# More rows by seven products in the head and MLP products of a one-core encoder layer, one more sum per half carried by transfers, and two raw weight buffers

## The chip, the core and the metric

The program runs on one core of a Trainium2 chip (trn2). TensorE (PE in the profile, PEld for its weight loads) multiplies, VectorE (DVE) and ScalarE (ACT) work on tiles, GpSimd (POOL) and SyncE (SP) issue transfers; ACT issues a few too. The metric is the device time of one execution in microseconds (us).

## What is computed

One layer over 256 tokens of width 2048, all in float32: a retention mixer of 8 heads, a squared-ReLU MLP with 8192 hidden columns, a norm ahead of each and one at the end.

```python
hn = rmsnorm(x, norm1)
q, k, v, g = split(hn @ w_in)              # 8 heads: 256, 256, 512, 512 columns each
q, k = rotary(q), rotary(k) * 256**-0.5
o = retention over chunks of 64 (q k^T, decayed, times v, with a carried state)
x = x + (head_norm(o) * silu(g)) @ w_out   # 4096 -> 2048
h2 = rmsnorm(x, norm2)
x = x + square(relu(h2 @ w_up)) @ w_down   # 2048 -> 8192 -> 2048
out = rmsnorm(x, final_norm)
```

## The kernel before, in words

**Weights.** A weight arrives in float32 from memory. It is split on the chip in two parts: ACT copies it into a rounded tile `wh` (L72, L155) and DVE subtracts that from the raw weight into `wl` (L73, L156). Activations are held as two parts in the same way. A product is three matmuls for each 128 x 512 block of weights: high by high, high by low, low by high. There are four pairs of `wh`/`wl` buffers of 1024 columns. ACT may write a pair only when TensorE has used what was in it, and DVE comes after ACT.

**Regular blocks.** `load_block` (L62 to L85) brings 1 MB (128 x 2048) from memory into a `raw` buffer by a transfer on SP's queue and splits it in two pairs. There are three raw buffers. In `seven` such a block is the step `r`: two rows of 128 of the weight matrix, 24 matmuls.

**Seven products.** `seven` computes a product with 256 tokens and 1024 output columns. Part of the weight's rows go in pairs by Strassen's scheme: the four quarters b11, b12, b22, b21 of the weight are loaded (step `w`, L207), and seven products of sums of quarters (steps `1` to `7`) take the place of eight. A product of n pairs is 3n matmuls, and n pairs by seven products are 21n, where regular blocks take 24n. The quarters are summed in place between the products, each sum once the quarter that it overwrites has been split for the product that still needs it: step `a` is b11 += b12, `b` is b12 += b22, `c` is b11 += b22, `d` is b21 += b11. A sum is a DVE addition (L202) or a transfer that adds, issued by POOL (L200). Products that belong to several blocks of the result are added from PSUM by DVE (`sub_out`, L718; `add_residual`, L586).

The order of work in each half of columns is written out by hand as a string of steps. The tile framework's scheduler then orders each engine's queue; each engine runs its queue in order.

**Stages.** Heads (0 to about 560 us): head 0 by regular blocks; for heads 1 to 7 first the queries and keys (`queries`, 4 blocks), then gates and values in one `seven` (3 pairs and 5 regular blocks, all four sums by DVE). Then the output product, two halves with 4 pairs. Then the MLP in four quarters of 2048 hidden columns; a quarter is 16 blocks of the first product (`proj_cols`, L97 and L98, results squared and split into `hs`) and two halves of the second product, each a `seven` with 4 pairs and 4 regular blocks: `rw1abr5cr26dr374`, sums `b` and `d` by transfers and `a` and `c` by DVE. The quarters b11, b12 and b22 live in the tile `raw3`, b21 in `raw1`; each holds one half's weights, so a quarter's next load waits for its last reader. In the very last half the final norm (`finish`) runs between the products.

Of the kernel before, what the change touches and what calls it, by code (L numbers as in the profile page):

```python
# [15 lines left out]
P = 128  # L16
T = 256
# [8 lines left out]
EPS = 1e-6  # L26
NB = T // P
WARM = 8
SPR = 3
SPO = 4  # L30
SPM = 4
QT = 16
STRASSEN_HEADS = range(1, 8)


@with_exitstack
def trunk_kernel(ctx: ExitStack, tc: tile.TileContext, io, out):
# [19 lines left out]
    def tiles(t):  # L57
        return [t[:, k] for k in range(t.shape[1])]

    def load_block(src, rows, cols, lead=None):  # L62
        raw = wp.tile([P, 2048], F32, tag="raw", name="raw", bufs=3)
        if lead is None:
            nc.sync.dma_start(raw, src)
        parts = []
        for s in range(2):
            wh = wp.tile([P, 1024], F32R, tag="wh", name="wh", bufs=4)
            wl = wp.tile([P, 1024], F32R, tag="wl", name="wl", bufs=4)
            r = raw[:, s * 1024 : (s + 1) * 1024]  # L70
            if lead is None:
                nc.scalar.copy(wh, r)  # L72
                nc.vector.tensor_sub(wl, r, wh.bitcast(F32))  # L73
            for k in range(rows // 2):
                sl = slice(k * cols, (k + 1) * cols)
                if lead is not None:
                    row = s * rows // 2 + k
                    lead(row)
                    nc.sync.dma_start(r[:, sl], src[:, row * cols : (row + 1) * cols])
                    nc.scalar.copy(wh[:, sl], r[:, sl])  # L80
                    nc.vector.tensor_sub(wl[:, sl], r[:, sl], wh[:, sl].bitcast(F32))
                parts.append((wh[:, sl], wl[:, sl]))
        return parts
# [56 lines left out]
    def seven(quads, blocks, raws, xs, sx, sub_out, done, order, side, extra=None, np_=SPR, nk=QT, by_dma=()):  # L140
# [34 lines left out]
        def total(i):  # L175
            return lambda p: (sx[p][:, i, 0], sx[p][:, i, 1])

        def out(b, c, acc, sign):
            sub_out(b, c, acc, sign, (b, c) not in taken)
            taken.add((b, c))  # L180
# [15 lines left out]
                    add(kt, wh, wl, b, range(2), kt == nk - 1)  # L196

        def plus(to, other):
            if to in by_dma:
                nc.gpsimd.dma_start(w[to], w[other], accum_op=ALU.add)  # L200
            else:
                nc.vector.tensor_add(w[to], w[to], w[other])  # L202

# [30 lines left out]
        def p7():  # L234
            chain = other["s"]
            product(chain, "s", w["b12"], total(2))
            out(1, 0, chain, 1)
            out(1, 1, chain, -1)

        steps = {"w": whole, "1": p1, "2": p2, "3": p3, "4": p4, "5": p5, "6": p6, "7": p7, **(extra or {})}  # L240

# [9 lines left out]

        finished = set()
        steps["A"] = lambda: finish_at((0, 0), (0, 1))
        steps["B"] = lambda: finish_at((1, 1))
        g = 0
        for step in order:
            if step == "r":
# [21 lines left out]
    xs = cp.tile([P, KT, 2, T], F32R, tag="xs", name="xs")  # L279

    xr = cp.tile([P, KT, T], F32, tag="ya", name="xr", padded_shape=[P, 32, T])
    sraw = cp.tile([P, 4, SPR * 512], F32, tag="yb", name="sraw")
    sxc = cp.tile([P, 2, 4, 2, P], F32R, tag="yc", name="sxc")
    x0 = tiles(xs)
    ys = [None] * VT

# [34 lines left out]
    if True:  # L321
# [74 lines left out]
        def queries(h, fillers):  # L396
            acc = [bank("acc_qk", 0) for _ in range(4)]
            proj_cols(io["w_qk"][h], x0, acc, fillers, (lambda w: st.update(first=w)) if h == 0 else None)
            qk = ap.tile([P, 2, 2, T], F32, tag="qk", name="qk")
            for i in range(2):  # L400
                both = []
                for o in (2 * i, 2 * i + 1):
                    a = ap.tile([P, T], F32, tag="sum", name="sum", bufs=3)
                    nc.scalar.copy(a, acc[o][:, T:])
                    nc.vector.tensor_add(a, acc[o][:, :T], a)
                    both.append(a)
                a1, a2 = both
                t = [ap.tile([P, T], F32, tag="rot", name="rot", bufs=4) for _ in range(4)]
                nc.vector.tensor_mul(t[0], a1, cosr)
                nc.vector.tensor_mul(t[1], a2, sinr)  # L410
                nc.vector.tensor_mul(t[2], a1, sinr)
                nc.vector.tensor_mul(t[3], a2, cosr)
                nc.vector.tensor_sub(qk[:, i, 0], t[0], t[1])
                nc.vector.tensor_add(qk[:, i, 1], t[2], t[3])
            st["qk"] = qk
# [66 lines left out]

        def sums_x():

            sx3 = ap.tile([P, 4, 2, P], F32R, tag="xh", name="sx3", bufs=2)
            to = [sxc[:, 0], sxc[:, 1], sx3]
            for p in range(SPR):
                s = []
                for k in (2 * p, 2 * p + 1):
                    s.append(ap.tile([P, T], F32, tag="sum", name="sum", bufs=3))  # L490
                    nc.scalar.activation(s[-1], xr[:, k], AF.Copy, scale=norm1[:, k : k + 1])
                k = 2 * SPR + 2 * p
                u = xr[:, k : k + 2].rearrange("p a (s t) -> p (a s) t", s=2)
                sums(to[p], s, u)
            st["sx"] = to

        def gates_values(h):

            sg = ap.tile([P, NB, DV], F32, tag="sg", name="sg")
            vf = ap.tile([P, NB, DV], F32, tag="xh", name="vf", bufs=2)  # L500
            v = ap.tile([P, NB, 2, DV], F32R, tag="v", name="v")
            to = (sg, vf)

            def sub_out(b, c, bank, sign, first):
                t = to[c][:, b]
                if first:
                    nc.scalar.copy(t, bank)
                else:
                    nc.vector.tensor_tensor(t, t, bank, op=ALU.add if sign > 0 else ALU.subtract)

            def done(acc, b, c):
                t = to[c][:, b]
                nc.vector.tensor_add(t, t, acc[b][c])
                if c == 0:
                    nc.scalar.activation(t, t, AF.Silu, scale=rs[:, b : b + 1])
                else:
                    split_scaled(v[:, b], t, rs[:, b : b + 1])

            i = h - STRASSEN_HEADS[0]
            seven(  # L520
                io["w_gv_s"][i], io["w_gv_r"][i], [sraw[:, j] for j in range(4)], x0, st["sx"],
                sub_out, done, "rwr1abr5cr2d3s6r74", 1, extra={"s": lambda: scores(h)},
            )
            st["sg"], st["v"] = sg, v

        for h in range(H):
            if h == 0:
                gates(h, [], lead=lead_x)
                queries(
                    h,  # L530
                    [(0, lambda: square_tokens(0, 0)), (0, lambda: square_tokens(0, 1)), (0, load_constants)]
                    + [(g, lambda g=g: square_tokens(1, g - 1)) for g in (1, 2)]
                    + [(3, first_norm), (3, gate_silu)],
                )
                values(h, [(0, lambda: load_decay(0)), (1, lambda: load_decay(1)), (1, sums_x), (2, lambda: scores(0))])
                ys_part("ya", 0, 16)
            else:

                queries(h, [(1, lambda: mix(h - 1))] + ([(3, lambda: turn(h - 1))] if h <= 4 else []))
                if h + 1 < H:  # L540
                    load_decay(h + 1)
                gates_values(h)
        ys_part("yb", 16, 12)
        ys_part("yc", 28, 4)


    mp = None
# [101 lines left out]


    hs = tiles(cp.tile([P, QT, 2, T], F32R, tag="ya", name="hs"))
    raw3 = cp.tile([P, 3, SPM * 512], F32, tag="yb", name="raw3")
    raw1 = cp.tile([P, SPM * 512], F32, tag="yc", name="raw1")
    rs3 = mp.tile([P, NB], F32, name="rs3")

    def times_norm(b, q):
# [3 lines left out]
    def finish(acc, b, half, c):  # L660
# [15 lines left out]
        if c != b:  # L676
            r = rs3[:, b : b + 1]
            for q in range(4):
                n = slice(q * 512, (q + 1) * 512)
                if q % 2:  # L680
                    nc.scalar.activation(x[:, b, n], x[:, b, n], AF.Copy, scale=r)
                    nc.scalar.dma_start(out[b * P : (b + 1) * P, n], x[:, b, n])
                else:
                    nc.vector.tensor_scalar_mul(x[:, b, n], x[:, b, n], r)
                    nc.sync.dma_start(out[b * P : (b + 1) * P, n], x[:, b, n])
# [6 lines left out]
    for q in range(4):  # L692
# [21 lines left out]
        for half in range(2):  # L714

            def sub_out(b, c, acc, sign, first, half=half):
# [2 lines left out]

            last = q == 3  # L720
            seven(
                io["w_down_s"][q][half], io["w_down_r"][q][half], [raw3[:, j] for j in range(3)] + [raw1], hs, sx, sub_out,
                (lambda a, b, c, half=half: finish(a, b, half, c)) if last
                else (lambda a, b, c, half=half: add_residual(a, half, b, c)),
                "rw1abr5cFr2d36rA7B4" if last and half == 1 else "rw1abr5cr26dr374",
                1 - half, np_=SPM, extra={"F": first_half_times_norm}, by_dma=("b12", "b21"),
            )


# [95 lines left out]
```

## Time and profile before

| | |
|---|---|
| median of 3 runs | 1445.39 us (1445.39 to 1446.39) |
| the profiled execution's own time | 1445.77 us |
| its span, first to last instruction | 1444.0 us |
| busy share of the span: PE, DVE, ACT, POOL | 99%, 78%, 56%, 3% |
| mean granted TensorE clock | 0.998 of full speed |
| read from memory | 277.18 MB, 193 GB/s over the span |

Busy time of an engine is a share of the whole span; a stage can be fuller. Matmuls are pipelined: one of 512 columns is listed with some 0.39 us, but the next starts 0.23 us after it. So the cost of a matmul more or less is taken from stretches of many in a row, not from the mean of one.

### The profile page before, as it was taken

To read this page: it belongs to the slowest core of one execution; us is meant where nothing else is said; L and a number is where in the kernel's file an instruction comes from. 1 tells how busy PE (TensorE), PEld (TensorE's weight loads), DVE (VectorE), ACT (ScalarE), POOL (GpSimd) and SP (SyncE) were. 2 spreads that over 40 slices of the span, in tenths; PEclk is the share of its full clock that TensorE was granted. 3 is DMA by queue.
4 is the path that set the end of the run, shared out by engine and by line. 5 is a ranking of instruction groups with operands and counts; after the bars stand their busy time and mean duration, and the time that the engine had idled before them with its cause. 6 is when DMAs were issued, how large, how long until landed. Compare 5 with 4: busy or idle time off the path is not lost.

```text
span 1444.0 us, 18258 instructions
## 1 busy us (share of the span) xinstructions
PE 1431.0 (99%) x6985; PEld 1196.8 (83%) x6985; DVE 1132.5 (78%) x1494; ACT 807.3 (56%) x1067; POOL 41.4 (3%) x66
## 2 busy tenths in 40 slices
PE   9999999999999999999999999999999999999996
PEld 7888888888888888888888888888888888888885
DVE  6768888888788888889568688777887678867787
ACT  5655564646464556555546555556555555556564
POOL 2000000000000000000000000000000000000000
PEclk9999999999999999999999999999999999999999
DMA  9845555546464636563475577754876557865773
GB/s 327 331 150 188 179 195 175 188 169 213 166 234 137 231 132 245 205 248 103 164 290 193 185 219 218 271 197 153 270 245 224 187 169 243 284 209 175 208 230 87
DMA packets 45863, 297.23 MB, mean 206 GB/s; under 512 B 5344, under 2 KB 5888, under 8 KB 13776
## 3 DMA queue, kind: packets, MB, share of 16 engines
q1 hardware_dynamic: 41184, 271.60, 53.2%
q0 software_dynamic: 3872, 23.42, 7.4%
q8 instruction: 54, 0.88, 0.2%
q10 hardware_dynamic: 720, 1.06, 0.2%
q14 instruction: 33, 0.27, 0.1%
HBM read 277.18 MB, written 2.10 MB: 193 GB/s over the span
## 4 chain that ended last, share of the span: by engine, by line
PE 98%; issue 0%; DMA 0%; ACT 0%; DVE 0%; POOLq 0%; POOL 0%; SPq 0%
PE acc_d L161 43%; PE acc_u L97 17%; PE acc_s L161 9%; PE acc_u L98 8%; PE acc_qk L97 8%; PE acc_qk L98 4%; PE acc L161 3%; PE po L456 1%; PE pst L433 1%; PE acc_g L112 1%; PE acc_g L113 1%; PE acc_g L116 1%; PE acc_v L116 1%; PE acc_v L113 1%; PE acc_v L112 1%; PE pt L478 0%
## 5 line engine op out<-in xcount | busy, mean ns | idle before, releaser
L73 DVE TENSOR_TENSOR wl<-raw,wh 128x1024 fp32r<-128x1024 f32 x382 | 463.6, 1222 | 204.9 <-ACT wh L72 202.8
L72 ACT CAST wh<-raw 128x1024 fp32r<-128x1024 f32 x382 | 398.9, 1050 | 369.3 <-PE acc_d L161 153.8
L97 PE MATMUL acc_u<-x1s,wh 128*128 128x512 f32 x1024 | 362.4, 398 | 0.0
L98 PE MATMUL acc_u<-x1s,wl 128*128 128x256 f32 x1024 | 287.6, 281 | 0.0
L97 PEld LDWEIGHTS acc_u<-x1s,wh 128*128 128x128 f32 x1024 | 192.5, 188 | 47.3
L161 PE MATMUL acc_d<-wh,xs 128*128 128x512 f32 x644 | 206.6, 393 | 0.0
L161 PE MATMUL acc_d<-wh,hs 128*128 128x512 f32 x640 | 205.8, 395 | 0.0
L98 PEld LDWEIGHTS acc_u<-x1s,wl 128*128 128x128 f32 x1024 | 192.2, 188 | 0.2
L97 PE MATMUL acc_qk<-xs,wh 128*128 128x512 f32 x512 | 181.2, 397 | 0.0
L156 DVE TENSOR_TENSOR wl<-raw,wh 128x1024 fp32r<-128x1024 f32 x112 | 135.0, 1222 | 39.1 <-ACT wh L155 38.9
L155 ACT CAST wh<-raw 128x1024 fp32r<-128x1024 f32 x112 | 117.3, 1049 | 84.8 <-PE acc_d L161 62.7
L161 PEld LDWEIGHTS acc_d<-wh,xs 128*128 128x128 f32 x644 | 121.0, 188 | 27.3 <-issue 0.7
L161 PEld LDWEIGHTS acc_d<-wh,hs 128*128 128x128 f32 x640 | 120.6, 188 | 27.3
L98 PE MATMUL acc_qk<-xs,wl 128*128 128x256 f32 x512 | 143.1, 281 | 0.0
L161 PE MATMUL acc_d<-wl,xs 128*128 128x512 f32 x322 | 126.1, 392 | 0.0
L161 PE MATMUL acc_d<-wl,hs 128*128 128x512 f32 x320 | 125.6, 394 | 0.0
L155 ACT CAST wh<-sraw 128x1024 fp32r<-128x1024 f32 x98 | 80.5, 835 | 72.7 <-PE acc_d L161 50.6
L97 PEld LDWEIGHTS acc_qk<-xs,wh 128*128 128x128 f32 x512 | 95.8, 188 | 22.7
L156 DVE TENSOR_TENSOR wl<-sraw,wh 128x1024 fp32r<-128x1024 f32 x98 | 91.3, 955 | 24.0 <-ACT wh L155 23.2
L98 PEld LDWEIGHTS acc_qk<-xs,wl 128*128 128x128 f32 x512 | 96.1, 188 | 2.2 <-DVE wl L73 1.2
L161 PEld LDWEIGHTS acc_d<-wl,hs 128*128 128x128 f32 x320 | 60.3, 188 | 13.8
L161 PEld LDWEIGHTS acc_d<-wl,xs 128*128 128x128 f32 x322 | 60.5, 188 | 13.3
(195 smaller groups left out, 1830.8 us busy)
## 6 DMA issues: line engine op xcount, KB each, us to landing
raw<-in_w_up SPq DMA_DIRECT2D x64, 1024.0 KB, 4.9
raw<-in_w_gv_r SPq DMA_DIRECT2D x35, 1024.0 KB, 5.0
raw<-in_w_qk SPq DMA_DIRECT2D x32, 1024.0 KB, 5.0
raw<-in_w_down_s SPq DMA_DIRECT2D x32, 1024.0 KB, 5.2
raw<-in_w_down_r SPq DMA_DIRECT2D x32, 1024.0 KB, 5.1
raw<-in_w_o_r SPq DMA_DIRECT2D x24, 1024.0 KB, 5.0
sraw<-in_w_gv_s SPq DMA_DIRECT2D x28, 768.0 KB, 4.2
raw<-raw POOLq DMA_DIRECT2D x16, 1024.0 KB, 8.2
```

The costliest lines, as they stand in the source:

```text
L72: nc.scalar.copy(wh, r)
L73: nc.vector.tensor_sub(wl, r, wh.bitcast(F32))
L97: nc.tensor.matmul(acc, wh[:, c], both, start=(kt == 0), stop=False)
L98: nc.tensor.matmul(acc[:, :T], wl[:, c], xs[kt][:, 0, :], start=False, stop=(kt == KT - 1))
L112: nc.tensor.matmul(accs[b][c], xs[kt][:, 0, t], wh[:, n], start=(kt == 0), stop=False)
L113: nc.tensor.matmul(accs[b][c], xs[kt][:, 0, t], wl[:, n], start=False, stop=False)
L116: nc.tensor.matmul(accs[b][c], xs[kt][:, 1, t], wh[:, n], start=False, stop=(kt == nk - 1))
L155: nc.scalar.copy(wh[:, :n], c)
L156: nc.vector.tensor_sub(wl[:, :n], c, wh[:, :n].bitcast(F32))
L161: nc.tensor.matmul(to, x, w, start=(key not in begun), stop=last, skip_group_check=True)
L433: nc.tensor.matmul(pst[:, to], qk[:, 1, i, b * P : (b + 1) * P], qk[:, 0, i, q], start=(i == 0), stop=(i == 1))
L456: nc.tensor.matmul(po, s, w, start=(n == 0), stop=(n == len(terms) - 1))
```

## The change

Heads 1 to 7: four pairs by seven products and four regular blocks (before: three and five), and step `b` goes to a transfer. Second MLP product: five pairs and three regular blocks in each half (before: four and four), quarters of 128 x 2560, and the sums `b`, `c` and `d` go by transfers (before: `b` and `d`), each in two pieces of 1280 columns (5120 bytes) a row. From head 1 to the end there are two raw buffers; in head 0 every third block takes the place that the heads' quarters use later. The last half finishes its blocks at other points. `rot` and `vf` share one buffer.

```diff
-SPR = 3
+SPR = 4
 SPO = 4
-SPM = 4
+SPM = 5
+DMA_ROW = 5120
+SUMS_BY_DMA = (("b12", "b22"), ("b11", "b22"), ("b21", "b11"))
...
+    blocks = {"n": 0, "third": (cp, "yb")}
+    def raw_tile():
+        blocks["n"] += 1
+        if blocks["third"] is not None and blocks["n"] % 3 == 0:
+            pool, tag = blocks["third"]
+            return pool.tile([P, 2048], F32, tag=tag, name="raw", padded_shape=[P, 8192])
+        return wp.tile([P, 2048], F32, tag="raw", name="raw", bufs=2)
     def load_block(src, rows, cols, lead=None):
-        raw = wp.tile([P, 2048], F32, tag="raw", name="raw", bufs=3)
+        raw = raw_tile()
...
         def plus(to, other):
-            if to in by_dma:
-                nc.gpsimd.dma_start(w[to], w[other], accum_op=ALU.add)
+            if (to, other) in by_dma:
+                nc.gpsimd.dma_start(w[to], w[other], accum_op=ALU.add, max_dma_last_dim=DMA_ROW if np_ > 4 else None)
             else:
                 nc.vector.tensor_add(w[to], w[to], w[other])
...
         def p7():
             chain = other["s"]
             product(chain, "s", w["b12"], total(2))
+            out(1, 1, chain, -1)
+            if "A" in order:
+                finish_at((1, 1))
             out(1, 0, chain, 1)
-            out(1, 1, chain, -1)
...
             seven(
-                io["w_gv_s"][i], io["w_gv_r"][i], [sraw[:, j] for j in range(4)], x0, st["sx"],
-                sub_out, done, "rwr1abr5cr2d3s6r74", 1, extra={"s": lambda: scores(h)},
+                io["w_gv_s"][i], io["w_gv_r"][i], sraws, x0, st["sx"],
+                sub_out, done, "rw1abr5cr2d3s6r74", 1, by_dma=SUMS_BY_DMA[:1], extra={"s": lambda: scores(h)},
             )
...
-                if q % 2:
+                if q % 2 or b == 0:
                     nc.scalar.activation(x[:, b, n], x[:, b, n], AF.Copy, scale=r)
                     nc.scalar.dma_start(out[b * P : (b + 1) * P, n], x[:, b, n])
...
-                "rw1abr5cFr2d36rA7B4" if last and half == 1 else "rw1abr5cr26dr374",
-                1 - half, np_=SPM, extra={"F": first_half_times_norm}, by_dma=("b12", "b21"),
+                "rw1abr5cFr26d3A74" if last and half == 1 else "rw1abr5cr26d374",
+                1 - half, np_=SPM, extra={"F": first_half_times_norm}, by_dma=SUMS_BY_DMA,
```

**DVE in a second half of the second MLP product.** `raw_6208` (before) and `raw_6079` (changed) are `raw3`, `raw_6209` and `raw_6080` are `raw1`; `wl<-raw` alone is a regular block. Before, from the first product (step `1`) to the products `2` and `6`:

```order
L156 TENSOR_TENSOR wl<-raw_6208,wh 128x1024 x2
L73 TENSOR_TENSOR wl<-raw,wh 128x1024
L202 TENSOR_TENSOR raw_6208<-raw_6208 128x2048
L73 TENSOR_TENSOR wl<-raw,wh 128x1024
L718 TENSOR_TENSOR x<-x,acc_s 128x512
L156 TENSOR_TENSOR wl<-raw_6208,wh 128x1024 x2
L202 TENSOR_TENSOR raw_6208<-raw_6208 128x2048
L73 TENSOR_TENSOR wl<-raw,wh 128x1024 x2
L718 TENSOR_TENSOR x<-x,acc_10357 128x512 x2
L156 TENSOR_TENSOR wl<-raw_6209,wh 128x1024 x2
L156 TENSOR_TENSOR wl<-raw_6208,wh 128x1024 x2
```

and changed:

```order
L168 TENSOR_TENSOR wl<-raw_6079,wh 128x1024 x2
L168 TENSOR_TENSOR wl<-raw_6079,wh 128x512
L214 TENSOR_TENSOR raw_6079<-raw_6079 128x2560
L85 TENSOR_TENSOR wl<-raw,wh 128x1024
L731 TENSOR_TENSOR x<-x,acc_s 128x512
L85 TENSOR_TENSOR wl<-raw,wh 128x1024
L168 TENSOR_TENSOR wl<-raw_6079,wh 128x1024 x2
L168 TENSOR_TENSOR wl<-raw_6079,wh 128x512
L85 TENSOR_TENSOR wl<-raw,wh 128x1024 x2
L731 TENSOR_TENSOR x<-x,acc_10331 128x512 x2
L168 TENSOR_TENSOR wl<-raw_6080,wh 128x1024 x2
L168 TENSOR_TENSOR wl<-raw_6080,wh 128x512
```

Each product has a third, half-full piece; sum `c` (the second L202) is gone from DVE.

**DVE at the end of such a half.** From the last product (step `4`, from `raw1`) into the next block's `wl<-raw`, before:

```order
L156 TENSOR_TENSOR wl<-raw_6209,wh 128x1024
L73 TENSOR_TENSOR wl<-raw,wh 128x1024
L718 TENSOR_TENSOR x<-x,acc_s 128x512 x2
L73 TENSOR_TENSOR wl<-raw,wh 128x1024
L586 TENSOR_TENSOR x<-acc_d,x 128x512 x2
```

and changed:

```order
L168 TENSOR_TENSOR wl<-raw_6080,wh 128x1024 x2
L731 TENSOR_TENSOR x<-x,acc_s 128x512 x2
L168 TENSOR_TENSOR wl<-raw_6080,wh 128x512
L599 TENSOR_TENSOR x<-acc_d,x 128x512
L85 TENSOR_TENSOR wl<-raw,wh 128x1024
L599 TENSOR_TENSOR x<-acc_d,x 128x512
```

The two additions of product `7` now stand ahead of the last piece of product `4` and of the next block's first piece, which was ahead of them.

**SP in the second MLP product.** From one quarter into the next, changed (`w_down_r` are regular blocks, `w_down_s` the quarters b11 to b21):

```order
L77 DMA raw<-in_w_down_r 128x2048 x5
L219 DMA raw_6079<-in_w_down_s 128x2560 x3
L219 DMA raw_6080<-in_w_down_s 128x2560
L77 DMA raw<-in_w_down_r 128x2048
L77 DMA raw<-in_w_up 128x2048 x2
L219 DMA raw_6079<-in_w_down_s 128x2560 x3
L219 DMA raw_6080<-in_w_down_s 128x2560
L77 DMA raw<-in_w_up 128x2048 x14
```

The four quarters of a half now follow each other, with the third `w_up` block behind them (before, it was ahead of three of them). On POOL, which issues nothing else there, the transfers of a half stand as `b`, `c`, `d` (before `b`, `d`).

## Rows read from the trace of the kernel before

**Rows 1.** The page: busy us (share of the span) and instructions of each engine.
```profile
PE 1431.0 (99%) x6985; PEld 1196.8 (83%) x6985; DVE 1132.5 (78%) x1494; ACT 807.3 (56%) x1067; POOL 41.4 (3%) x66
```
**Rows 2.** The waits of PE, longest of three rows: us in total, times, longest.
```profile
PE pw L305 <- DVE mhalf L298: 1.1, 1, 1.1
...
```
**Rows 3.** The chain in order of time, a second half: start us, us, what.
```profile
1040.61 8.40 PE acc_d L161 x36
1049.01 2.80 PE acc_s L161 x12
1051.81 5.60 PE acc_d L161 x24
...
1060.20 8.26 PE acc_d L161 x36
1068.46 2.80 PE acc_s L161 x12
```
**Rows 4.** The same chain in a head's gates and values.
```profile
273.87 5.51 PE acc_d L161 x24
279.38 2.07 PE acc_s L161 x9
```
**Rows 5.** Stretches: us, busy PE, PEld, DVE, ACT, POOL, PEclk, DMA share, GB/s.
```profile
1000.00:1086.00 86.00, 86.00 (x377) 69.93 (x376) 75.74 (x79) 50.80 (x57) 3.38 (x4) 1.00 0.77 241
...
236.00:306.00 70.00, 70.00 (x343) 58.39 (x342) 56.60 (x75) 39.29 (x52) 1.69 (x3) 1.00 0.53 184
```
**Rows 6.** The timeline of DVE in the same second half: start us, us, instruction.
```profile
1048.48 2.28 DVE L202 TENSOR_TENSOR raw<-raw 128x2048 f32<-128x2048 f32 x1
...
1054.84 2.29 DVE L202 TENSOR_TENSOR raw<-raw 128x2048 f32<-128x2048 f32 x1
```
**Rows 7.** The timeline of POOL there: start us, us, instruction [idle before].
```profile
1051.29 0.85 POOL L200 DMA_DIRECT2D raw<-raw  x1 [28.23 <-DVE raw L202]
```
**Rows 8.** Line L200, all 16 issues: ns min/median/max, and to landing.
```profile
L200 POOL DMA_DIRECT2D raw<-raw x16: 834/844/916, 834.4 to 1413.3; - x16
...
DMA to landing us min/median/max: 6.9/8.2/10.7
```
**Rows 9.** Transfer issues, 1050 to 1064 us: count, KB each, median us to landing.
```profile
raw<-in_w_up SPq DMA_DIRECT2D x2, 1024.0 KB, 7.2
raw<-raw POOLq DMA_DIRECT2D x1, 1024.0 KB, 10.0
```
**Rows 10.** Stretches as rows 5: a sum alone; a sum and a block; loads alone.
```profile
1024.00:1028.00 4.00, 4.00 (x19) 3.25 (x18) 2.62 (x3) 3.10 (x3) 0.00 (x0) 1.00 0.97 197
1056.00:1060.00 4.00, 4.00 (x19) 3.24 (x18) 3.50 (x3) 2.11 (x2) 0.00 (x0) 1.00 1.11 295
1076.00:1080.00 4.00, 4.00 (x19) 3.24 (x18) 2.86 (x4) 2.41 (x3) 0.00 (x0) 1.00 1.00 424
```
**Rows 11.** Groups by form: busy us, mean ns of one, idle before.
```profile
L155 ACT CAST wh<-raw 128x1024 fp32r<-128x1024 f32 x112 | 117.3, 1049 | 84.8 <-PE acc_d L161 62.7 <-PE acc_u L97 7.1 <-PE acc L161 5.6
...
L156 DVE TENSOR_TENSOR wl<-raw,wh 128x1024 fp32r<-128x1024 f32 x112 | 135.0, 1222 | 39.1 <-ACT wh L155 38.9
...
L202 DVE TENSOR_TENSOR sraw<-sraw 128x1536 f32<-128x1536 f32 x28 | 49.2, 1756 | 0.7
...
L202 DVE TENSOR_TENSOR raw<-raw 128x2048 f32<-128x2048 f32 x16 | 36.6, 2286 | 0.1
...
L156 DVE TENSOR_TENSOR wl<-sraw,wh 128x512 fp32r<-128x512 f32 x49 | 33.7, 688 | 6.5 <-ACT wh L155 6.5
...
L718 DVE TENSOR_TENSOR x<-x,acc_s 128x512 f32<-128x512 f32 x32 | 21.1, 681 | 0.0
```
**Rows 12.** The timelines of PE and DVE at the end: last matmul, last additions.
```profile
1432.59 0.40 PE L161 MATMUL acc_d<-wh,hs 128*128 128x512 f32 x1
...
1433.62 1.28 DVE L586 TENSOR_TENSOR x<-acc_d,x 128x512 f32<-128x512 f32 x2
```

More of the change, by code (lines that the diff above doesn't have):

```diff
@@ L253, in seven @@
         steps["A"] = lambda: finish_at((0, 0), (0, 1))
-        steps["B"] = lambda: finish_at((1, 1))
         g = 0
@@ L281, in trunk_kernel @@
     xr = cp.tile([P, KT, T], F32, tag="ya", name="xr", padded_shape=[P, 32, T])
-    sraw = cp.tile([P, 4, SPR * 512], F32, tag="yb", name="sraw")
-    sxc = cp.tile([P, 2, 4, 2, P], F32R, tag="yc", name="sxc")
     x0 = tiles(xs)
@@ L407, in queries @@
                 a1, a2 = both
-                t = [ap.tile([P, T], F32, tag="rot", name="rot", bufs=4) for _ in range(4)]
+                t = tiles(ap.tile([P, 4, T], F32, tag="rot", name="rot"))
                 nc.vector.tensor_mul(t[0], a1, cosr)
@@ L483, in sums_x @@
         def sums_x():
-            sx3 = ap.tile([P, 4, 2, P], F32R, tag="xh", name="sx3", bufs=2)
-            to = [sxc[:, 0], sxc[:, 1], sx3]
+            to = [ap.tile([P, 4, 2, P], F32R, tag="xh", name="sxa", bufs=2) for _ in range(2)]
+            to += tiles(ap.tile([P, SPR - 2, 4, 2, P], F32R, name="sxb"))
             for p in range(SPR):
@@ L499, in gates_values @@
             sg = ap.tile([P, NB, DV], F32, tag="sg", name="sg")
-            vf = ap.tile([P, NB, DV], F32, tag="xh", name="vf", bufs=2)
+            vf = ap.tile([P, NB, DV], F32, tag="rot", name="vf")
             v = ap.tile([P, NB, 2, DV], F32R, tag="v", name="v")
@@ L536, in trunk_kernel @@
                 ys_part("ya", 0, 16)
+                blocks["third"] = None
+                sraw = cp.tile([P, 4, SPR * 512], F32, tag="yb", name="sraw")
+                sraws = [sraw[:, j] for j in range(4)]
             else:
@@ L542, in trunk_kernel @@
                 gates_values(h)
-        ys_part("yb", 16, 12)
-        ys_part("yc", 28, 4)
+        ys_part("yb", 16, 16)
     mp = None
@@ L651, in trunk_kernel @@
     hs = tiles(cp.tile([P, QT, 2, T], F32R, tag="ya", name="hs"))
-    raw3 = cp.tile([P, 3, SPM * 512], F32, tag="yb", name="raw3")
-    raw1 = cp.tile([P, SPM * 512], F32, tag="yc", name="raw1")
+    raw3 = cp.tile([P, 3 * SPM * 512], F32, tag="yb", name="raw3", padded_shape=[P, 8192])
+    raw1 = mp.tile([P, SPM * 512], F32, name="raw1")
     rs3 = mp.tile([P, NB], F32, name="rs3")
@@ L721, in trunk_kernel @@
             seven(
-                io["w_down_s"][q][half], io["w_down_r"][q][half], [raw3[:, j] for j in range(3)] + [raw1], hs, sx, sub_out,
+                io["w_down_s"][q][half], io["w_down_r"][q][half], [raw3[:, j * SPM * 512 : (j + 1) * SPM * 512] for j in range(3)] + [raw1], hs, sx, sub_out,
                 (lambda a, b, c, half=half: finish(a, b, half, c)) if last
                 else (lambda a, b, c, half=half: add_residual(a, half, b, c)),
-                "rw1abr5cFr2d36rA7B4" if last and half == 1 else "rw1abr5cr26dr374",
-                1 - half, np_=SPM, extra={"F": first_half_times_norm}, by_dma=("b12", "b21"),
+                "rw1abr5cFr26d3A74" if last and half == 1 else "rw1abr5cr26d374",
+                1 - half, np_=SPM, extra={"F": first_half_times_norm}, by_dma=SUMS_BY_DMA,
             )
```

## The prediction

> **What bounds the kernel now.** I read the page first: PE is busy for 1431.0 of 1444.0 us [rows 1]. The waits of PE confirm that nothing holds it in the middle: its longest wait is 1.1 us, at the start [rows 2]. So every matmul less shortens the kernel, and every wait of PE that the change makes lengthens it. Next, how near the others are in the stages that are touched. In the two halves of a second MLP product DVE is busy for 75.74 of 86 us and the transfer engines for 0.77 of the time; in a head DVE for 56.60 of 70 us and the transfers for 0.53 [rows 5]. In the MLP neither has much room.
>
> The price of a matmul I take from the chain: 24 in 5.60 us in the MLP, 0.233 each [rows 3]; 24 in 5.51 us in a head, 0.230 each [rows 4].
>
> **The change, part by part.** All sums are made against the profiled execution: span 1444.0 us, own time 1445.77, which is 0.4 above the median of 1445.39.
>
> *Matmuls.* A pair by seven products is 21 matmuls, by regular blocks 24. One more pair in 7 heads saves 21 x 0.230 = 4.8 us, one more in 8 MLP halves 24 x 0.233 = 5.6 us. All of it is on the path: **-10.4 us**.
>
> *Heads.* DVE's splits and sums were 10 of 1.22 us for the regular blocks, 7 x (1.22 + 0.69) for three pairs and 4 sums of 1.76, 32.6 us; now 8 of 1.22, 14 of 1.22 and 3 sums of 2.29, 33.7 us [rows 11]. One us more per head hides in DVE's 13 idle us [rows 5]. Sum `b` by a transfer takes some 8 us to land [rows 8] and is needed only at product 7, two regular blocks and four products later, some 20 us. The raw blocks have one buffer less, but a block is needed about 5 us after the one before it is used up and lands in some 5 (7.2 in company [rows 9]); TensorE works on pairs split earlier meanwhile. I take 0; between nothing and 0.3 us a head, 2 us. The extra sums of activations (one pair in head 0, one in each MLP quarter) lie beside the first products, where DVE waits for buffers: 0.
>
> *DVE in an MLP half.* Four regular blocks become three (2 x 1.22 less), seven products have a third piece of 0.69 each, sum `a` grows from 2.29 to about 2.8 (0.53 per 512 columns, from 1.76 to 2.29 [rows 11]), sum `c` goes (2.29 less): +0.6 us. As a total this is covered. Its order is another matter (end of a half, below).
>
> *Sum `c` as a transfer.* Here the change adds a wait. Product 6 is computed from b11 after `c`, so ACT's cast of its first piece waits for `c` to land; every later cast is queued behind it, DVE's subtraction behind ACT and TensorE behind both. I work out one second half, with 0 at TensorE's first regular block (1043.4: 12 of the 36 matmuls that start at 1040.61 belong to the last product [rows 3]). With 5.6 us for a block and 3.5 for a product of 15 matmuls, product 6 is due at 3 x 5.6 + 3 x 3.5 = **27.3**.
>
> The issue of `b` came at 7.9 [rows 7], behind the sum `a`, which ran from 5.1 to 7.4 [rows 6]. `a` is 0.5 us longer but now stands ahead of the regular block's first subtraction; I keep 7.9. `c` can be issued when product 5 is split. Behind `a`, from 7.9 on, DVE has the second regular block's two pieces, one result and three pieces of product 5, 4 x 1.14 + 2 x 0.6 (the pitch of such instructions in a row is some 0.08 under their durations): 13.7 (before, the sum `c` on DVE began at 11.4 [rows 6]). So `c` is queued behind `b`.
>
> How long the transfer engines work on a sum: alone it moves 197 GB/s at a share of 0.97 [rows 10], so 1.05 MB takes 5.2 us of them, 1.7 less than the shortest landing of 6.9 [rows 8]. A plain block runs at 424 GB/s [rows 10], 2.5 us. A sum of 1.31 MB is 6.45 us. With a block in its way a sum lands in 10.0 instead of 6.9 [rows 8, 9]: the block's time is added, nothing overlaps. Two blocks are asked for in this stretch: with two raw buffers, one when the second regular block is split (7.9 + 1.14 + 0.6 + 1.14, about 11), one when the third is (its last piece gets its buffers when TensorE has used product 5's first piece, 14.7 + 1.4, and needs 2.3 for cast and subtraction: about 18).
>
> The engines therefore have b 6.45 + block 2.5 + c 6.45 + block 2.5 = 17.9 us of work from `b` on. `c` lands at 7.9 + 1.7 + 17.9 = 27.5; without the second block in its way at 25.0. Cast 1.05, subtraction 1.22 and some 0.2 of hand-over come behind it: product 6 can start at 30.0, or 27.5. TensorE waits between 0.2 and 2.7 us. I take **2.5**: the second block is asked for some 7 us before `c` would be done alone, and the row nearest to it, the 10.0, shows that a block does go in between. First halves are alike (`b` was issued 6.4 after their start and is some 1.5 later now, behind the results of the first product). 8 x 2.5 = **+20 us**.
>
> *Sum `d`* follows `c`: issued at 27.8, landed at 27.8 + 1.7 + 6.45 = 36. Product 4 is due 10.5 us after product 6, at 40.5, and its pieces must be there 2.5 earlier, at 38. No further wait; if `c` came later, both shift alike. b11's next load waits for `d`, but 9 us are left before it is split again.
>
> *The end of a half.* DVE now adds product 7's two results ahead of product 4's last piece, then another result, then splits the next block. Product 7 ends at x; DVE adds from x + 0.2 (2 x 0.6), splits the last piece (0.6), adds (0.6), splits the next block (1.14, the pitch of such instructions in a row): ready at x + 3.8, where TensorE is through with product 4 at x + 3.5. So 0.3 us in time, and when DVE comes late, because product 6 began with no piece ahead, about 1.0 (the same five instructions, begun 0.7 later, behind product 4's second piece). I take 1.0, **+8 us**; 0.3 without the wait for `c`.
>
> *The very end.* The last product's second piece now stands behind three additions that wait for product 7: about 1.8 us of waiting for TensorE. Behind the last matmul, three of the four additions that followed it (1432.6 to 1434.9 [rows 12]) are gone, 1.3 to 1.8 us. **+0.5**, between -1.5 and +2.
>
> **Sum:** -10.4 + 20 + 8 + 0.5 = +18.1. Span 1462.1, own time 1463.9; against the median **1463.5 us**.
>
> **A rule against the row.** All 16 issues of sums by POOL took 0.834 to 0.916 us [rows 8], though DVE was busy throughout most of these stretches (3.50 of 4.00 us beside one of them [rows 10]). So I put no wait for DVE into the three issues of a half.
>
> The Trainium skill ("SBUF — State Buffer", section "SBUF: two separate sides") says that GpSimd and VectorE share a port pair under an exclusive lock, so that GpSimd cannot write a transfer's descriptors while certain VectorE instructions run. [...]
>
> **Rivals.** *A, `c` in time* (ends on the other side). The second block's data come behind `c`, or `b` starts a little earlier: `c` at 25.0 instead of 27.5. The point that decides is 24.9, 2.4 us ahead of product 6. Then 8 x (0.2 + 0.3) = 4 us of waits at most stand against 10.4: span 1434 to 1438, with the end 1440; own time from 1435 to 1441. For it: both bounds of `c` lie close to the point, and I stacked every block in its way. Against it: the 10.0 us.
>
> *B, half late.* One of the two blocks passes, and `c` lands about 1.2 late: 8 x (1.2 + 0.4) = 13 against 10: 1445 to 1449, no change that could be told.
>
> *C, raw blocks late as well.* In each quarter the third block of the next first product now waits behind all four quarters' loads, 4 x 3.1 us (5.24 MB at 424 GB/s): 1 to 2 us in each of four quarters, some 6 us on top of A or of the forecast. For it: the order of SP; against it: the block is needed only 11 us into the stage.
>
> *D, the lock on POOL's issues*, worked out as a mechanism here: each of 8 issues of `c` behind one DVE instruction, 1.2 to 2.8 us later, 10 to 22 us on top of the forecast: 1474 to 1486. Against it: the 0.916 us. [...]
>
> **How the numbers follow.** Forecast 0.50; its own range is 1453 (half of the waits for `c`) to 1471 (0.7 more on every landing, as 10.7 against 10.0 [rows 8], is 6 us, and 2 in the heads). A 0.33, B 0.09, C 0.05 (on top of the forecast, mostly), D 0.03. Less than 0.2%, 2.9 us, is about what a measurement of this kernel can tell from no change. Faster: A and a third of B, 0.36; same: the rest of B, 0.06; slower: the forecast, C and D, 0.58. The range from 1435 to 1471 reaches from the whole saving of A to the forecast with its landings late; it leaves out D and a part of C.
>
> **What would show it.** In the changed trace: MLP matmuls in stretches of 15 at the same pitch; ACT's cast of product 6's first piece idle for the transfer, eight times, with TensorE waiting about 2.5 us there; `c` landing 13 us or so after its issue; a second, shorter wait of TensorE at the start of each next block, for DVE. Heads without waits. It is wrong if `c` lands within 10 us of its issue: then TensorE has no wait at product 6 and A holds. It is wrong in another place if TensorE waits in the heads or for a `w_up` block.

## The result: slower by 3.8%, and the profile after

The changed kernel takes **1499.74 us** (median of 4 runs, 1498.92 to 1500.93) against 1445.39 (4 runs, 1444.89 to 1446.39): a ratio of 1.0378, 95% interval 1.0364 to 1.0391. The forecast was 1463.5 with a range from 1435 to 1471: the sign was right, the size was not.

The page of the changed kernel, first part (engine, busy time, share of the span, instructions):

```profile
span 1498.8 us, 18302 instructions
## 1 busy us (share of the span) xinstructions
PE 1441.3 (96%) x6940; PEld 1197.8 (80%) x6940; DVE 1143.2 (76%) x1528; ACT 830.6 (55%) x1102; POOL 62.5 (4%) x81
```

Against [rows 1], PE has fewer instructions and more busy us, and still a smaller share of the span: some matmuls ran slowly, and there are gaps between them. The waits of TensorE (engine, tile, line, releaser: total us, times, longest) and ScalarE's for the transfers:

```profile
PE acc_s L173 <- ACT wh L167: 32.8, 8, 5.3
PE acc_s L173 <- DVE wl L168: 4.7, 9, 0.8
PE acc_u L110 <- DVE wl L85: 2.3, 3, 0.8
PE acc_d L173 <- DVE wl L168: 2.0, 1, 2.0
PE acc_u L109 <- ACT wh L84: 1.9, 2, 1.1
...
ACT wh L167 <- DMA raw<-raw: 69.1, 9, 9.7
```

The kernel before had next to none of these [rows 2]. `acc_s` at L173 for L167's cast is product 6, eight times, as forecast; behind it stands ScalarE's wait for the transfers of sums. The second half of the MLP's first quarter, which runs from 873.8, step by step; first the three issues of sums on GpSimd (start, duration, then the idle time before), the raw blocks on SP's queue, and the cast of product 6's first piece:

```profile
882.58 1.19 POOL L212 DMA_DIRECT2D raw<-raw  x1 [25.02 <-ACT wh L84]
888.19 1.19 POOL L212 DMA_DIRECT2D raw<-raw  x1 [4.43 <-DVE wl L168]
904.88 1.19 POOL L212 DMA_DIRECT2D raw<-raw  x1 [15.50 <-DMA raw<-raw]
```

```profile
885.04 7.71 SPq L77 DMA_DIRECT2D raw<-in_w_up  x2
```

```profile
904.45 3.46 ACT L167 CAST wh<-raw 128x1024 fp32r<-128x1024 f32 x4 [8.88 <-DMA raw<-raw]
```

`b` is issued 8.8 us after the half's start, `c` at 14.4, two raw blocks are asked for from 11.2 to 18.9, and `c` has landed at 30.6. TensorE then:

```profile
905.55 0.80 PE L173 MATMUL acc_s<-wh,sx 128*128 128x512 f32 x1 [4.46 <-ACT wh L167]
906.81 0.80 PE L173 MATMUL acc_s<-wl,sx 128*128 128x512 f32 x1 [0.46 <-DVE wl L168]
907.40 1.06 PE L173 MATMUL acc_s<-wh,sx 128*128 128x512 f32 x2
908.25 0.63 PE L173 MATMUL acc_s<-wl,sx 128*128 128x512 f32 x1
...
910.89 0.63 PE L173 MATMUL acc_s<-wh,sx 128*128 128x512 f32 x2
911.36 0.39 PE L173 MATMUL acc_s<-wl,sx 128*128 128x512 f32 x1
```

It waits 4.46 and 0.46 us, and then the matmuls start 0.43 us apart, not 0.23, until 910.7. The same place in stretches (busy us of PE, PEld, DVE, ACT, POOL; granted clock; DMA share; GB/s) says why:

```profile
902.00:904.00 2.00, 0.00 (x0) 0.00 (x0) 0.00 (x0) 0.00 (x0) 0.00 (x0) 0.91 0.68 135
904.00:906.00 2.00, 0.45 (x1) 0.29 (x1) 0.47 (x1) 1.55 (x2) 1.11 (x1) 0.50 0.00 0
906.00:908.00 2.00, 1.54 (x4) 1.01 (x4) 2.00 (x3) 1.91 (x3) 0.07 (x1) 0.50 0.80 143
908.00:910.00 2.00, 2.00 (x7) 1.54 (x6) 2.00 (x3) 0.65 (x1) 0.00 (x0) 0.50 1.06 184
910.00:912.00 2.00, 2.00 (x9) 1.63 (x8) 1.46 (x2) 1.02 (x2) 0.00 (x0) 0.89 0.97 172
```

While TensorE did nothing its granted clock fell from 1.00 to 0.50 (2.4 to 1.2 GHz) and came back only after some 7 us. This happened in seven of the eight halves. In the eighth no raw blocks are left to load; there product 6 waits 0.20 us for the cast, and the clock stays at 1.00.

The 54.8 us between the two spans (1444.0 and 1498.8), by the starts of the first matmuls of each stage and the waits in it:

| part | forecast, us | measured, us |
|---|---|---|
| head 1 to the output projection (480.07 before, 475.62 after) | -4.8 | -4.5 |
| head 0 and output projection | 0 | +1.7 |
| 24 matmuls fewer in the MLP's halves | -5.6 | -5.6 (taken; below) |
| TensorE's waits at product 6 | +20 | +37.2 |
| slow clock behind seven of them, 2.5 each | not seen | +17.4 |
| ends of halves; up projections of quarters 2 to 4 | +8 | +5.4 |
| rest of the last half and the end | +0.5 | +3.1 |

The 2.5 is what is left of the lengthening in the first three quarters: their halves took 292.4 us against 250.3 before, 42.1 more; less 31.3 of waits, plus the 4.2 saved on matmuls, leaves 14.9 for six falls. Not all of it is the clock's: a wait costs some 0.2 us beyond its listed length (in c_transfer_alone's second quarter, below, four waits of 2.7 us together made the halves 3.7 us longer with no fall), so some 0.4 of the 2.5 belongs to the two waits of a half.

### The profile page after: what moved, and what is told of

Same layout as the page of the kernel before. It is cut to its first block, busy times and chain, and to the rows that moved or that the text cites. A ratio compares the mean times of both kernels' runs of the same rounds, so it can differ in the third digit from the quotient of the medians.

```text
span 1498.8 us, 18302 instructions
## 1 busy us (share of the span) xinstructions
PE 1441.3 (96%) x6940; PEld 1197.8 (80%) x6940; DVE 1143.2 (76%) x1528; ACT 830.6 (55%) x1102; POOL 62.5 (4%) x81
## 5 line engine op out<-in xcount | busy, mean ns | idle before, releaser
L84 ACT CAST wh<-raw 128x1024 fp32r<-128x1024 f32 x352 | 365.5, 1050 | 305.7 <-PE acc_d L173 93.8
L167 ACT CAST wh<-raw 128x1024 fp32r<-128x1024 f32 x168 | 147.8, 905 | 144.1 <-DMA raw<-raw 69.1
L173 PE MATMUL acc_d<-wh,xs 128*128 128x512 f32 x560 | 179.2, 392 | 0.0
L173 PE MATMUL acc_d<-wh,hs 128*128 128x512 f32 x544 | 170.8, 393 | 0.0
L167 ACT CAST wh<-sraw 128x1024 fp32r<-128x1024 f32 x98 | 102.5, 1053 | 77.1 <-PE acc_d L173 45.1
L168 DVE TENSOR_TENSOR wl<-sraw,wh 128x1024 fp32r<-128x1024 f32 x98 | 117.9, 1221 | 27.6 <-ACT wh L167 26.5
L173 PEld LDWEIGHTS acc_d<-wh,xs 128*128 128x128 f32 x560 | 105.2, 188 | 23.9 <-issue 0.7
L173 PEld LDWEIGHTS acc_d<-wh,hs 128*128 128x128 f32 x544 | 102.3, 188 | 22.6
L173 PE MATMUL acc_d<-wl,xs 128*128 128x512 f32 x280 | 109.0, 392 | 0.0
L173 PE MATMUL acc_s<-wh,sx 128*128 128x512 f32 x192 | 75.2, 460 | 32.8 <-ACT wh L167 32.8
L173 PE MATMUL acc_d<-wl,hs 128*128 128x512 f32 x272 | 103.6, 393 | 2.7 <-DVE wl L168 2.0
L173 PEld LDWEIGHTS acc_s<-wh,sx 128*128 128x128 f32 x192 | 43.4, 226 | 46.4 <-ACT wh L167 36.3
```

The lines of the kernel that those rows point to most:

```text
L167: nc.scalar.copy(wh[:, :n], c)
L168: nc.vector.tensor_sub(wl[:, :n], c, wh[:, :n].bitcast(F32))
L173: nc.tensor.matmul(to, x, w, start=(key not in begun), stop=last, skip_group_check=True)
```

## Experiments

Theories at the start: **T1**, the transfer of `c` is late, queued behind `b` and with raw blocks in its way, and the clock's fall behind the wait costs on top; **T2**, two raw buffers make blocks late; **T3**, five pairs load VectorE too much.

**c_by_dve.** Only `c` goes back to VectorE.

```diff
-                1 - half, np_=SPM, extra={"F": first_half_times_norm}, by_dma=SUMS_BY_DMA,
+                1 - half, np_=SPM, extra={"F": first_half_times_norm}, by_dma=(SUMS_BY_DMA[0], SUMS_BY_DMA[2]),
```

> The changed kernel with one thing undone: in the eight MLP halves the sum c runs on VectorE again (about 2.8 us each); b and d stay transfers, the five pairs, the two raw buffers and the new end stay. Theory T1 (the transfer of c, queued behind that of b and with raw blocks in its way, makes product 6 wait, and the fall of the granted clock behind that wait costs as much again): no TensorE wait for ACT's cast at product 6 over 1 us, no stretch at a granted clock of 0.5 inside the MLP, time 1435 to 1442 us, faster than the kernel before. Theory T2 (two raw buffers make the regular blocks late): the time stays above 1470. Theory T3 (five pairs load VectorE so that its pieces come late, whichever engine sums): waits move to VectorE's subtractions, 1450 to 1480.

Measured 1447.02 us, ratio to the kernel before 1.0008 (0.9999 to 1.0017). Its waits:

```profile
PE acc_d L173 <- DVE wl L85: 5.3, 5, 2.2
PE acc_u L109 <- ACT wh L84: 1.9, 3, 1.2
PE acc_g L124 <- ACT wh L92: 1.8, 3, 1.0
PE acc_d L173 <- DVE wl L168: 1.8, 1, 1.8
```

No wait at product 6 is left: `c`'s transfer, with the slow clock behind its waits, costs 52.7 us. In the first three quarters the two halves take 82.11, 81.74 and 81.84 us against 83.44 before, so the matmuls' 1.4 a quarter are there. But the time missed its 1435 to 1442, so something takes the gain back: the output projection is 2.7 us longer than before (three waits of 2.4 us together for VectorE's splits of regular blocks), the up projections of quarters 2 to 4 are 0.9 to 2.1 longer (`acc_u` waits for a `w_up` block), and the last quarter's halves lose 6.3 us. In the very last half VectorE has the 2.8 us of `c`, results and the multiplications `F` ahead of a regular block, TensorE waits 2.2 us, and the clock falls behind that wait as well (0.59 in 1412 to 1416). In this small part T3 holds.

**heads_alone** and **two_raw**: one part alone each, timed with the run above. heads_alone keeps the heads of the change and sets `SPM = 4` with the kernel before's sums, orders and end.

```diff
-SPM = 5
+SPM = 4
...
-                "rw1abr5cFr26d3A74" if last and half == 1 else "rw1abr5cr26d374",
+                "rw1abr5cFr2d36rA7B4" if last and half == 1 else "rw1abr5cr26dr374",
```

> Only the heads' part of the change (four pairs by seven products, b by a transfer, two raw buffers from head 1 on); the second MLP product and the end as in the kernel before. T1: the heads gain their 4.8 us of matmuls and nothing waits, 1440 to 1442 us. T2: two raw buffers make blocks late in the heads or the MLP, above 1446. T3 says nothing of the heads.

Measured 1442.53 us, ratio 0.9979 (0.9970 to 0.9988). From head 1 to the output projection it takes 475.81 us, 4.3 less than before, with no wait; the output projection is 0.9 longer, where a block is late once.

two_raw is the kernel before with `bufs=2` for the raw buffers.

> The kernel before with two raw buffers in place of three throughout, and nothing else. T1: the third buffer hides nothing that counts, within 2 us of 1445.4. T2: 10 us or more slower. A smaller loss, 2 to 6 us, would be a term of its own that the sum took as 0 to 2 us.

Measured 1455.63 us, ratio 1.0071 (1.0059 to 1.0084): some 10 us, T2's number. But of the profiled run's 9.5 us, 8.7 are in head 0, which the changed kernel gives a third buffer:

```profile
PE acc_qk L97 <- ACT wh L72: 4.9, 1, 4.9
```

```profile
36.00:40.00 4.00, 0.00 (x0) 0.00 (x0) 0.00 (x0) 1.49 (x3) 0.05 (x1) 1.00 1.01 416
40.00:44.00 4.00, 2.75 (x8) 2.00 (x9) 1.79 (x3) 3.11 (x5) 1.02 (x2) 0.60 0.54 193
44.00:48.00 4.00, 4.00 (x15) 3.48 (x14) 3.18 (x3) 3.58 (x6) 0.00 (x0) 0.54 0.83 262
```

One wait of 4.9 us (0.6 more right behind it), and the clock at half speed behind it again. From head 1 to the end 0.9 us are lost, 0.6 of them in the output projection, with no wait over 0.3. So T2 as the main cause falls; what two buffers cost in the output projection is settled by third_raw below.

**c_before_b.** The order asks for `c` ahead of `b` (`"rw1ar5cbr26d374"`).

> The changed kernel with b's transfer asked for behind c's in every MLP half (order 1 a r 5 c b r 2 6 d 3 7 4). T1, in the form that c's place in the queue behind b is what makes it late: c lands 8 to 11 us after its issue, 5 us or more earlier than now, product 6 waits under 1 us, and b, needed 7 us later by product 7, waits 0 to 2 us: 1440 to 1455. T1 in the form that the transfer engines are full (three sums and three blocks and four loads in a half, whatever their order): the 4 to 5 us wait and the clock at 0.5 stay, at product 7 or 4 in place of 6, 1480 to 1505. T2 and T3: no change, 1490 to 1505, with the wait at product 6.

Measured 1499.0 us, 1.0372 (1.0358 to 1.0386). It tells nothing of the order: the scheduler that places the instructions put the issues on GpSimd's queue as they were, and the run shows only that the result repeats (32.9 us of waits at product 6).

**b_by_dve.** The same question, by a way that leaves no choice: `b` on VectorE, so that `c` is first in the queue.

```diff
-                1 - half, np_=SPM, extra={"F": first_half_times_norm}, by_dma=SUMS_BY_DMA,
+                1 - half, np_=SPM, extra={"F": first_half_times_norm}, by_dma=SUMS_BY_DMA[1:],
```

> The changed kernel with the MLP's sum b on VectorE (2.8 us more of it in a half) and c and d by transfers, so that c is the first sum in GpSimd's queue. Theory Q (c is late because it is queued behind b): c lands 8 to 11 us after its issue instead of 16, its issue comes 1 to 3 us later since VectorE sums b first, product 6 waits 0 to 2.5 us instead of 4 to 5, at most half of the stretches at a clock of 0.5 are left: 1445 to 1470. Theory F (the transfer engines are full, whatever the order): c still lands some 30 us after the half's start, wait and slow clock stay, 1490 to 1510.

Measured 1482.65 us, 1.0258 (1.0242 to 1.0274): above Q's range and below F's, for a new reason. The waits, then `c`'s issue and the cast that waits for it in the second half of the first quarter:

```profile
PE acc_d L173 <- DVE wl L85: 17.5, 10, 3.1
PE acc_s L173 <- ACT wh L167: 5.3, 4, 1.8
```

```profile
886.68 1.18 POOL L212 DMA_DIRECT2D raw<-raw  x1 [32.75 <-DVE wl L168]
```

```profile
898.53 3.47 ACT L167 CAST wh<-raw 128x1024 fp32r<-128x1024 f32 x4 [6.20 <-DMA raw<-raw]
```

`c` lands 11.9 us after its issue, not 16.3, and product 6's waits fall from 32.8 to 5.3 us. Q holds in its mechanism, though 11.9 us is over its 8 to 11: 4.4 of the 16.3 us went with `b` and the raw block that ran beside it. What is gained goes to VectorE, which splits regular blocks late behind the sum `b` (2.50 us in each first half).

**fewer_blocks.** The changed kernel, whose second and third regular block of a half are not loaded; the first block's data are split again in their place, so it leaves out part of the weights.

```diff
...
-            for j, (wh, wl) in enumerate(load_block(blocks[g], 2, 1024)):
+            for j, (wh, wl) in enumerate(load_block(blocks[g], 2, 1024, again=np_ > 4 and g > 0)):
...
```

> The changed kernel without the loads of the second and third regular block of each MLP half: ScalarE and VectorE split the first block's raw data again in their place (so those two blocks of the product carry wrong weights; the work on the engines is the same). The second raw buffer is then filled early, and one block instead of two is asked for while the transfer engines have b and c. Theory B (each block adds its 2.5 us to the landing of c): the wait at product 6 falls from 4 to 5 us to about 2, c's landing from some 30.6 us after the half's start to 28; 1470 to 1485. Theory G (c is late only through b ahead of it and the gap between the two sums): the waits stay over 3.5 us and the time over 1490.

Measured 1474.97 us (a single run). Issue and cast:

```profile
884.06 1.19 POOL L215 DMA_DIRECT2D raw<-raw  x1 [4.67 <-DVE wl L171]
```

```profile
896.98 2.51 ACT L170 CAST wh<-raw 128x1024 fp32r<-128x1024 f32 x3 [5.46 <-DMA raw<-raw]
```

`c` lands 12.9 us after its issue instead of 16.3; SP's queue shows one `w_up` block asked for behind `b`'s issue (at 888.39) where the changed kernel has two. The one beside `b` is gone: `b` lands 9.4 us after its issue instead of 11.7, which is 2.3 of the 3.3 us. Product 6 waits 9.5 us for the cast in all instead of 32.8. Theory B holds. The Trainium skill ("DMA: Bandwidth & Descriptors", section "Queues, rings and completion order") says that a transfer engine takes packets from its queues in turn; the trace agrees, since a block asked for later is served amid a sum (in the half shown, packets of the second block from 896.4 to 902.9, of `c` from 894.6 to 904.1).

**c_transfer_alone.** The kernel before with `c` as a third transfer, and four pairs as before.

```diff
-            if to in by_dma:
+            if to in by_dma or (to, other) == ("b11", "b22") and "b11c" in by_dma:
...
-by_dma=("b12", "b21"),
+by_dma=("b12", "b11c", "b21"),
```

> The kernel before with the MLP's sum c as a third transfer in each half, in 2048-element rows as its b and d, and nothing else: four pairs, four regular blocks, three raw buffers. If c's place behind b is the cost, whatever the number of pairs: b and c of 1.05 MB take 10 us each with a block in the way and stand one behind the other, product 6 waits 2 to 4 us in most halves and the clock falls behind the longer waits: 1470 to 1495. If it is the fifth pair (larger sums, less time before product 6) that makes c late: no wait over 1 us, 1443 to 1448.

Measured 1467.62 us (1461.32 to 1470.46), 1.0158 (1.0143 to 1.0174). The time lies between the two expectations. Smaller sums are late too, though less than expected; the profiled run:

```profile
PE acc_s L161 <- ACT wh L155: 6.0, 7, 1.3
PE acc_s L161 <- DVE wl L156: 5.3, 7, 0.8
```

So it is the place behind `b`, and the fifth pair makes it worse. After seven waits of 0.3 to 1.3 and 0.8 us the clock fell once (0.57 in 856 to 860) in this run, the fastest of the four. The other three runs, 6 to 9 us longer, left no trace; that they had more falls fits their mean granted clock, 0.993 to 0.994 against 0.997.

**dose.** Does the clock need the transfers in order to fall? heads_alone, with waits made by ScalarE alone: the first cast of product 6 is repeated 1 to 8 times more, in the eight halves in turn.

```diff
...
-                nc.scalar.copy(wh[:, :n], c)
+                for _ in range(casts if p0 == 0 else 1):
+                    nc.scalar.copy(wh[:, :n], c)
...
```

> The kernel with the heads' part alone (1442.5 us), in which ScalarE casts the first piece of product 6 again k times, 1.0 us each, with k = 1 to 8 in the eight MLP halves in turn: waits of TensorE of growing length at the same place, with no transfer behind them. Theory W (the wait itself makes the clock fall, whatever it is for): the short waits leave the granted clock at 1.00, the long ones (4 us and more surely) are followed by a stretch at 0.50 of some 7 us that costs 2.5 to 3.5 us: 1470 to 1485 in all. Rival (the clock falls through the transfers' traffic): the clock stays at 1.00 in all eight halves and the time is 1442.5 plus the waits alone, 1455 to 1470.

Measured 1475.63 us (a single run). The longest wait of TensorE in halves 4, 5, 6 and 7, and the stretches behind:

```profile
1068.13 0.50 PE L174 MATMUL acc_s<-wl,sx 128*128 128x512 f32 x1 [0.76 <-DVE wl L169]
...
1202.71 0.53 PE L174 MATMUL acc_s<-wh,sx 128*128 128x512 f32 x1 [1.63 <-ACT wh L168]
...
1251.82 0.80 PE L174 MATMUL acc_s<-wh,sx 128*128 128x512 f32 x1 [2.73 <-ACT wh L168]
...
1391.89 0.79 PE L174 MATMUL acc_s<-wh,sx 128*128 128x512 f32 x1 [3.78 <-ACT wh L168]
```

```profile
1068.00:1072.00 4.00, 3.87 (x17) 3.17 (x18) 4.00 (x6) 2.06 (x2) 0.00 (x0) 1.00 0.43 123
1204.00:1208.00 4.00, 4.00 (x10) 3.14 (x11) 3.32 (x3) 1.05 (x1) 0.00 (x0) 0.50 0.46 133
1252.00:1256.00 4.00, 3.53 (x8) 2.45 (x9) 4.00 (x4) 0.38 (x1) 0.00 (x0) 0.50 0.21 37
1392.00:1396.00 4.00, 3.53 (x8) 2.44 (x9) 4.00 (x4) 0.31 (x1) 0.00 (x0) 0.50 0.24 33
```

W holds: the clock stays at 1.00 in the first four halves, falls in the last four, and so a wait that ScalarE makes brings it down just as well, also where the transfer engines are nearly idle (a share of 0.01 in 1388 to 1392). In the third quarter the halves took 13.1 us more than in heads_alone, with 6.7 us of waits: 3.2 us more for each fall; in the fourth, 18.1 with 12.1, 3.0 each (here three waits go with each fall). The Trainium skill ("TensorE: Matmul & The Clock Gate", section "HAM oscillation — how this bites in real kernels") describes a kernel that loses its clock behind every wait for a transfer; the runs agree (a fall in seven of the eight halves of the changed kernel), and dose shows that the wait's cause does not matter.

**p3_before_6.** Would more time for `c` have helped? Product 3 is computed ahead of product 6 in all halves.

```diff
-                "rw1abr5cFr26d3A74" if last and half == 1 else "rw1abr5cr26d374",
+                "rw1abr5cFr236dA74" if last and half == 1 else "rw1abr5cr236d74",
```

> The changed kernel with product 3 computed ahead of product 6 in all eight halves: c and its way are the same, but product 6 is due 3.5 us later, and product 4, which waits for d behind c, 3.5 us sooner after it. If a short wait costs only itself: product 6 waits 0.5 to 1.8 us, product 4 waits 1 to 3 us for d, 1455 to 1465. If every wait brings the stretch of 0.5 with it: two such stretches in a half instead of one, 1490 or more. If only the long ones do: none at product 6, some at product 4, 1455 to 1480.

Measured 1520.52 us, 1.0520 (1.0505 to 1.0534):

```profile
PE acc_d L173 <- ACT wh L167: 30.3, 9, 8.8
PE acc_s L173 <- ACT wh L167: 7.4, 7, 1.5
PE acc_s L173 <- DVE x L731: 6.1, 6, 1.2
```

Product 6 does wait 0.4 to 1.5 us only for the cast, as worked out, but product 4 waits for `d` 1.9 to 4.0 us, 8.8 in one half, and the clock falls behind that in every quarter. Three more of the nine falls come behind product 6, after waits of only 0.8 to 1.5 and 0.8 us. The third row I had not seen: products 6 and 7 share an accumulator, and with nothing between them product 7 waits until VectorE has read product 6's result. The lateness of the queue was moved, not removed.

**both_parts** and **third_raw**, the two attempts at a better kernel. both_parts is c_by_dve with the last half in another order (`"rw1abr5cr2dF36A74o"`, `d` on VectorE there, product 7's results, `o`, behind product 4's first pieces).

> The heads' part and five pairs together without the late sums: c on VectorE in all halves; in the last half d on VectorE too, the order 1 a r 5 c r 2 d F 3 6 A 7 4, and the results of product 7 taken behind product 4's first pieces. Expected from the parts: the quarters' ends as in the kernel with c on VectorE up to the last one, and the 7 us that its last quarter lost to a wait of 2.2 us, one of 1.8 us and the slow clock behind them mostly back: 1438 to 1443. If five pairs cost VectorE more than TensorE gains, 1445 or more.

Measured 1444.92 us, 0.9996 (0.9987 to 1.0005): no difference from the kernel before. The last quarter's halves are still 3.9 us longer, with 3.4 us of small waits, the up projections lose 1.0 to 2.0 us in each of three quarters, and the output projection is 1.5 us longer.

third_raw is heads_alone with a third raw buffer again once the heads' memory is given back:

```diff
...
+        blocks["third"] = (mp, "raw_third")
...
```

> The kernel with the heads' part alone, with a third raw buffer again from the output projection's second half of weights on (where the memory of the heads has been given back). If the two raw buffers cost what TensorE waits for blocks in the output projection (0.9 us there), 1441 to 1442 us; if nothing, 1442.5; if more is hidden in the MLP, below 1441.

Measured **1441.03 us**, 0.9967 (0.9955 to 0.9980), the fastest here. From head 1 on TensorE waits 0.3 us in all, and the output projection takes 178.08 us against 179.69: 1.6 us were the price of two buffers there.

## Why the prediction was right in sign and wrong in size

- **Heads, -4.8:** right; -4.5, and no wait there. `b` as a transfer is hidden.
- **Matmuls of the MLP, -5.6:** right; c_by_dve shows them where nothing else disturbs.
- **Product 6 is due at 27.3 after the half's start:** right (901.1 in the half shown). The blocks were asked for at 11.2 and 18.6 (about 11 and 18 in the text), `c` at 14.4 (13.7).
- **`c` lands at 27.5:** this is the first step that failed; it was 30.6. `b` was issued some 0.9 us later than in [rows 7]. The other 2.2 lie in the term for the sums: from `b`'s issue to `c`'s landing I gave 1.7 + 17.9 = 19.6 us, and it took 21.8. The last half, where no load runs beside them, measures the sums alone (the issues of `b` and `c`, and the cast that waits for `c`):

```profile
1452.62 1.18 POOL L212 DMA_DIRECT2D raw<-raw  x1 [26.82 <-issue]
1458.39 1.18 POOL L212 DMA_DIRECT2D raw<-raw  x1 [4.59 <-DVE wl L168]
1470.46 3.47 ACT L167 CAST wh<-raw 128x1024 fp32r<-128x1024 f32 x4 [4.73 <-DMA raw<-raw]
```

That is 17.8 us, where the forecast's terms without blocks give 1.7 + 6.45 + 6.45 = 14.6. So the two sums were given some 3 us too little, and the two blocks 1.0 too much (4.0 us, from 17.84 to 21.87, against 5.0). One sum with nothing beside it lands 9.4 us after its issue, the least of all sums of the changed kernel, not 1.7 + 6.45 = 8.15:

```profile
DMA to landing us min/median/max: 9.4/11.6/16.9
```

So the time of a sum of 1.05 MB was scaled wrongly to 1.31 MB; why it grows by more than its bytes is not shown.
- **A wait of 2.5 us, eight times:** 4.3 to 5.8 in seven halves, 1.0 in the last, where no block is in the way; 37.2 us instead of 20.
- **A wait costs its own length:** this was never written down, and it is the larger mistake of kind: the slow matmuls behind a wait were put at nothing without a reason. They add 2.5 us to a half (3.0 to 3.2 for each fall in dose), 17.4 us in all. In dose waits of 1.6 and of 2.7 us (each with one of 0.6 us shortly before) brought the clock down too, in b_by_dve one of 2.50 us did so in one case of four; so the forecast's own 2.5 us might have drawn it in some halves. [Rows 1 to 5] hold no such wait, but the end of the trace before, where TensorE runs dry, was there to be read: its granted clock is 0.60 in 1436 to 1440 and 0.50 in 1440 to 1444.
- **End of a half, +8:** did not come; VectorE waits less than I stacked. One wait of 0.76 us at a regular block is all.
- **Rival C** was given 0.05 as some 6 us on top of the forecast, and came: 5.4 us in the up projections of quarters 2 to 4 (92.82, 91.49 and 92.46 us against 90.45).
- **Very end, +0.5:** TensorE waits 1.98 us for the last product's second piece (1.8 forecast), and what follows the last matmul is 9.5 instead of 11.4 us. The last half's other waits (3.1 us with this one) are in the +3.1 too; some 1 to 2 us of it no row accounts for, and the granted clock is 1.00 throughout that half.
- **Rival D, a lock on GpSimd's issues:** no. The 24 issues took 1.18 to 1.20 us each, 17 of them beside an instruction of VectorE. All of these combine two tensors (additions, subtractions, multiplications); this trace has no other kind there.

"Slower" had 0.58 of the chances and came, but the range's upper end stacked 0.7 us on a landing and nothing on the price of a wait. With 5.2 us for the wait and 2.5 for the clock in seven halves and 1.0 in the eighth, the same sum gives 1498. That it then comes so close is in part luck: its 8 us at the ends of halves did not come, and the 5.4 us in the up projections were not in it.

## What to carry to other kernels

A wait that is new on a saturated TensorE is to be priced with the slow matmuls behind it: here waits of some 4 to 6 us cost another 2.5 each, and shorter ones did so now and then. Work moved from an engine to transfers needs the queue's own sum, issue by issue, with each transfer that can slip in between; three sums, four loads and three blocks in a half left no room for a sum with a deadline. And parts of a change should be timed apart: here the heads' part gained 3.4 us (4.7 with a third buffer), and one sum by transfer lost 53.

## What was not expected of the hardware

- The granted clock falls to 0.50 during or right behind waits of TensorE, whoever makes it wait, and stays there for 6.8 us in the changed kernel; by the clock records of the traces, falls in b_by_dve and c_by_dve lasted 3.4 us too, and one behind a wait of 5.94 us in dose 10.2. It is no sharp line: in b_by_dve a wait of 2.50 us at the same place of the four quarters was followed by 0.73 in the first and by 1.00 in the three others; and waits of 0.94 and 0.76 us at the start of an up projection there were followed by 0.75 (928 to 932), where 1.12 and 0.76 us in the changed kernel left 1.00 (934 to 938).
- A sum's transfer of 1.31 MB takes 1.18 us to issue on GpSimd, one of 1.05 MB some 0.84 us [rows 8]. Of two sums in the queue, the second one's first packets came 1.0 us after the first one's last (893.6 and 894.6 in the half shown, by the packets of the trace).
